# A two-layer decoder trunk on one core: the order and the engines of the block inverses, POOL as a second engine for low parts, halves at the start and in a LayerNorm

## The chip, the cores and the metric

The kernel runs on one core of a Trainium2 chip. The metric is the device time of one execution in microseconds (us). The engines are PE (TensorE, matmuls), DVE (VectorE), ACT (ScalarE), POOL (GpSimd) and SP (SyncE, which here only issues DMAs).

## The reference, cut to what matters

x is 256 tokens of 1024 channels, float32. Layer A is a gated DeltaNet mixer, layer B a MoBA attention; with 256 tokens and blocks of 256 the latter is plain causal attention. Each ends in a LayerNorm over `ALPHA * x + y`.

```python
proj = h @ w_in                                  # q, k, v, z, b, a
qkv = silu(causal_depthwise_conv(qkv, conv_w))   # 4 taps
g = -exp(a_log) * softplus(a + dt_bias);  beta = sigmoid(b)
lower = where(strict, (k_beta @ k.T) * decay, 0.0)
w, u = triangular_solve(eye + lower, ...)        # the inverse that the kernel forms
...                                              # recurrence over chunks of 64
o = o * rsqrt(mean(o**2) + eps) * norm_w * silu(z)
x = layer_norm(ALPHA * x + o @ w_out, g, b)
kb, vb = split(x @ w_kv);  q, z = split(x @ w_in_b)
y = (causal_attention(q, kb, vb) * silu(z)) @ w_out_b
x = layer_norm(ALPHA * x + y, g_b, b_b)
```

## The kernel before, in words

**Weights.** Every weight matrix comes in units of 128 x 1024 numbers (512 KB), 78 of them beside the z columns that the kernel starts with. `load_raw` loads a unit on SP's queue into one of 5 buffers. `high` casts it on ACT to the short format of PE's fast mode (hi); `low` subtracts on DVE (lo = raw - hi), frees the raw buffer and issues the next load. A projection makes three matmuls for each chunk of 128 input channels: hi with hi, hi with the low part of the other operand, lo with hi. `splits` decides when a unit's hi and lo are made, by how far ahead of use they are (RANKS); 9 units of hi and lo are kept. A unit of q, k or v holds one head of 128 columns, and columns 0 to 511 of the unit are its chunks 0 to 3.

**The order of the work.** A planner writes all instructions out at build time. `Clock` keeps a modelled time per engine, for DMA queues and for each tile; `Pipeline` holds chains, generators that yield the engine of their next step and what it needs, and places a step of a chain between the matmuls of the projections when its operands are there in modelled time. On the chip the order of each engine is then fixed, and semaphores carry the real waits. `SPINE` is the order of the projections: z columns 0 to 255 with the gate columns, q and k of 8 heads, v, the rest of z. POOL's two-operand instructions on most tiles are costed at 800 + 190 ns per column, those on tiles named inv at 155 + 1.75 per column.

**Start.** x and the first z columns are loaded in five pieces on two queues (SP, ACT), then the constants, then five raw units. `z_first` multiplies them in plain float32. `x_part` splits x into hi and lo, a piece at a time. `gates` works out g and beta in some twenty short steps on DVE; the products with g (ps_gc) stand in PE's order behind it. `decay` makes the decay matrices E, `conv` the four taps and silu, `gs_head` the products of keys and queries of a head and their scaling into M; POOL stores M to DRAM (md).

**Inverses.** `inverse(grp)` is started for each group of four heads once its four stores are issued. POOL loads the 16x16 diagonal blocks from md to inv, takes a root of the key norms (nk), clears a tile (TR), sets the identity, forms 64 block inverses by 15 steps of a product and a sum, stores them (td), and SP loads them back in eight transfers into TC. Then PE merges the blocks to 32, 64 and 128 with bursts of small matmuls: ps_x and ps_y of 32x32 (64 and 128 matmuls), later larger ones. Between them six copies on POOL bring the 32-blocks into RR and T64. `solve` and `read_out` use the result; og is scaled by zs, the silu of z.

**End of layer A.** The output projection runs by group of heads (`out_half`, k = 0 and 1), token tile t and column half c, in that order; `ln` is added after both halves of t with k = 1: a residual add and bn_stats for each half, bn_aggr, a root on POOL, scaling, shift; `x1_done` transposes on PE and splits x1 into hi and lo, which the values of layer B (`bv`) need.

Of the kernel before, what the change touches and what calls it, by code (L numbers as in the profile page):

```python
# [24 lines left out]
P = 128  # L25
# [21 lines left out]
R_KQ, R_V, R_Z, R_INV, R_SOLVE, R_ATT, R_BZ = 5, 5, 2, 2, 2, 5, 1  # L47
INVERSE = [('gpsimd', 'p'), ('gpsimd', 'p')]
START = 650.0
WARM = 9  # L50
# [59 lines left out]
class Clock:  # L110
# [44 lines left out]
    def note(self, ins):  # L155
# [22 lines left out]
        else:  # L178
# [14 lines left out]
            elif eng == mybir.EngineType.DVE:  # L193
                psum = any(a.tensor.name.startswith("ps_") for a in reads)
                single = ins.opcode in ("TensorCopy", "TensorScalarPtr") and len(reads) - bool(scalars) == 1
                cost = 68 + scalars + n * (6 if ins.opcode == "Reciprocal" else 0.52 if single and not psum else 1.042)
            elif ins.opcode == "TensorTensor":
                cost = 155 + 1.75 * n if ins.outs[0].bass_ap.tensor.name.startswith("inv") else 800 + 190 * n
            else:
                cost = 100 + n  # L200
# [106 lines left out]
def body(ctx, tc, x, xt, cst_in, w0, wp, a_ln_g, a_ln_b, b_ln_g, b_ln_b, out):  # L307
# [45 lines left out]


    specs, idx = [], {}
    for key, _, _, nk, _, n in granules():
# [8 lines left out]
    raws, hls, lows_due = {}, {}, []  # L365
    n_raw, n_split, n_used = [2], [2], [0]

    def load_raw():
        u = n_raw[0]
        raws[u] = rot(wraw, [P, 1024], F32, "raw", f"raw{u}", NR)  # L370
        n_raw[0] += 1
        nc.sync.dma_start(raws[u], wp[u - 2])

# [11 lines left out]
    def low():  # L385

        u, hi, lo = lows_due.pop(0)
        nc.vector.tensor_sub(lo, raws.pop(u), f32(hi))
        if n_raw[0] < len(units):
            load_raw()  # L390

    def rank(u):
# [3 lines left out]
    def splits():  # L396

        r = []
        if lows_due:
            u, hi, _ = lows_due[0]  # L400
            r.append((rank(u), pipe.idle("v") and pipe.there(hi, "v"), low))
        u = n_split[0]
# [62 lines left out]
    alog = cst_sb[:, 105:113].unsqueeze(1)  # L465
    pieces = [slice(0, 1), slice(1, 2), slice(2, 4), slice(4, 6), slice(6, 8)]
    for k in pieces:
        nc.sync.dma_start(x_sb[:, k], xt[:, k])
        nc.scalar.dma_start(zraw[:, k], w0[:, k])
    nc.sync.dma_start(cst_sb, cst_in)  # L470
    for _ in range(NR):
        load_raw()
# [53 lines left out]
    def x_part(hi, lo, raw):  # L526
        yield "a", [raw]
        nc.scalar.copy(hi, raw)
        yield "v", [hi]
        nc.vector.tensor_sub(lo, raw, f32(hi))  # L530

    for k in pieces:
        pipe.add(x_part(xh[:, k], xl[:, k], x_sb[:, k]), 0)
    pipe.others = splits

# [159 lines left out]

    n_md = [0, 0]
    n_gs = [0]
# [6 lines left out]
    def inverse(grp):  # L704
        inv = act.tile([64, 4, 16, 16], F32, tag="ag" if grp == 0 else "ab", name=f"inv{grp}")
        mb, tr, prod = inv[:, 0], inv[:, 1:3], inv[:, 3]
        blk = md[grp, 0, 0:16, 0:16]
        nc.gpsimd.dma_start(mb, bass.AP(tensor=blk.tensor, offset=blk.offset,
                                        ap=[[16 * (P + 1), 64]] + list(blk.ap)))
        nc.gpsimd.tensor_tensor(fl(nk)[:, 8 * grp:8 * grp + 8], fl(ssk)[:, 8 * grp:8 * grp + 8],  # L710
# [9 lines left out]
        nc.gpsimd.memset(t16, 0.0)  # L720
        nc.gpsimd.memset(t16.rearrange("p a b -> p (a b)")[:, 0::17], 1.0)
        eng, e = INVERSE[grp]
        eng = getattr(nc, eng)
        yield e, [inv]
        for j in range(15):
# [5 lines left out]
            if j in (4, 9):  # L731
                yield e, [t16]
        eng.tensor_copy(tr[:, 1], t16.rearrange("p a b -> p b a"))
        yield "p", [inv]
        nc.gpsimd.dma_start(td[grp].rearrange("w q b r c -> (q b) w (r c)"),
                            tr.rearrange("p w r c -> p w (r c)"))
        yield "p", [td[grp]]
        for b in range(8):
            nc.sync.dma_start(TC.rearrange("p w q c -> p (w q) c")[16 * b:16 * b + 16, :, 16 * (b % 2):16 * (b % 2) + 16],
                              td[grp].rearrange("w q b r c -> b r (w q) c")[b])  # L740
# [26 lines left out]
        for b in blocks:  # L767
            nc.gpsimd.tensor_copy(RR[b, :, b], TC[b, 1])
            if b.start < 64:
                nc.gpsimd.tensor_copy(T64[b, :, b], TC[b, 0])  # L770

# [73 lines left out]
    def z_rest(ps, c, t):  # L845
        yield "a", [ps[:, 0:256], lambda: n_E[0] == H]
        nc.scalar.activation(zs[:, t, c * 256:(c + 1) * 256], ps[:, 0:256], AF.Silu)
        end(ps)


# [3 lines left out]
    o_hl = {}  # L854
    n_ro = [0]
    n_s3 = [0, 0]
    n_og = [[0, 0], [0, 0]]
# [36 lines left out]
    def read_out(grp, t, hs, Wg, Z, nw):  # L894
# [20 lines left out]
        nc.gpsimd.tensor_tensor(a, a, nhalf[:, 0:4], op=ALU.pow)  # L915
        yield "v", [a, free("og")]
        og = rot(tmp, [P, 4, P], F32, "og", "og", 2)
# [30 lines left out]
    def z_keep(ps, t):  # L948
        z = zs[:, t, 0:256]
        yield "a", [ps[:, 0:256]]  # L950
        nc.scalar.copy(z, ps[:, 0:256])
        yield "a", [lambda: n_ba[0] == NT]
        end(ps)
        yield "a", [z, lambda: n_E[0] == H]
        nc.scalar.activation(z, z, AF.Silu)

    pipe.add(taps(), 3)
# [104 lines left out]

    oh.g = ol.g = 1
    for t in range(NT):
        pipe.wait(lambda: n_og[1][t])
        for c in range(2):
            pipe.run(out_half("o", 1, ps_y, t, c, oh, ol))
        pipe.add(ln([(ps_y[t, c], halfs[c]) for c in range(2)], halfs, "res", t, "x1", x1_done(t)), 2 + t)

# [166 lines left out]
```

## Time and profile before

| | us |
|---|---|
| median of 3 runs | 306.08 (306.07 to 307.4) |
| profiled execution, its own time | 307.82 |
| its span | 306.1 |
| PE, DVE, ACT, POOL busy | 292.2, 201.8, 162.6, 67.4 |
| granted clock, mean | 0.987 |

The span runs from the first to the last instruction of the profiled execution. Busy time counts neither waits nor the issue of DMAs by SP and ACT. A granted clock of 1.0 is 2.4 GHz, 0.5 is 1.2 GHz. Nearly all instructions are recorded by one helper, line 219, so groups go by the names of tiles.

### The profile page before, as it was taken

What the parts mean: (1) busy time and instruction counts of PE and PEld (TensorE: products, weight loads), DVE (VectorE), ACT (ScalarE), POOL (GpSimd) and SP (SyncE); (2) the same over time, 40 slices, a digit from 0 to 9 for tenths busy, and PEclk for the clock granted to TensorE, in tenths of its full rate; (3) what the DMA queues carried; (4) which work ended last, traced back from release to release, by engine and by line L of the source; (5) the groups of instructions that cost most, each with busy time, mean ns of one, the idle gap of its engine ahead of it and who ended that gap; (6) DMA issues with size and microseconds to landing.
All of it is one profiled execution on the core that took longest, in us unless ns stands there. A gap on an engine that the chain in (4) does not pass through costs nothing. (4 is left out here: it accounts for less than half of the span.)

```text
span 306.1 us, 6559 instructions
## 1 busy us (share of the span) xinstructions
PE 292.2 (95%) x2598; PEld 268.2 (88%) x2598; DVE 201.8 (66%) x432; ACT 162.6 (53%) x327; POOL 67.4 (22%) x137
## 2 busy tenths in 40 slices
PE   7899999999996999999999999999999999999990
PEld 6798988999996999997888678899999999998890
DVE  0589479999995285554455994765655656762645
ACT  2588987556572567455362524875555558561000
POOL 7002410188822988014011110000000000000101
PEclk9999999999999799999999999999999999999996
DMA  6985516565859353433528261796444546400011
GB/s 212 382 306 171 185 34 206 173 204 176 264 139 332 113 158 121 103 114 110 166 98 326 88 206 47 256 317 204 140 132 145 152 160 240 139 0 2 0 69 69
DMA packets 19309, 49.42 MB, mean 161 GB/s; under 512 B 6256, under 2 KB 7152, under 8 KB 19280
## 3 DMA queue, kind: packets, MB, share of 16 engines
q1 hardware_dynamic: 18016, 46.46, 45.8%
q0 software_dynamic: 544, 1.44, 1.8%
q10 hardware_dynamic: 720, 1.11, 1.0%
q8 instruction: 20, 0.33, 0.4%
q14 instruction: 9, 0.07, 0.1%
HBM read 46.65 MB, written 2.36 MB: 160 GB/s over the span
## 5 line engine op out<-in xcount | busy, mean ns | idle before, releaser
L219 DVE TENSOR_TENSOR lo<-raw,hi 128x1024 fp32r<-128x1024 f32 x78 | 95.4, 1230 | 20.9 <-ACT hi L219 20.6
L219 ACT CAST hi<-raw 128x1024 fp32r<-128x1024 f32 x78 | 80.6, 1049 | 15.1 <-DMA raw<-in_wp_dram 7.7
L219 PE MATMUL ps_y<-hi,o 128*128 128x512 f32 (+1 forms) x144 | 43.7, 376 | 0.0
L219 PE MATMUL ps_bkq<-x1h,hi 128*128 128x256 f32 x128 | 38.0, 297 | 0.0
L219 PE MATMUL ps_kq<-xh,hi 128*128 128x256 f32 x128 | 36.7, 287 | 0.0
L219 PE MATMUL ps_kq<-xh,lo 128*128 128x256 f32 x128 | 35.8, 279 | 0.8 <-DVE lo L219 0.8
L219 PE MATMUL ps_kq<-xl,hi 128*128 128x256 f32 x128 | 35.7, 279 | 0.0
L219 PE MATMUL ps_bkq<-x1l,hi 128*128 128x256 f32 x128 | 35.6, 278 | 0.0
L219 PE MATMUL ps_bkq<-x1h,lo 128*128 128x256 f32 x128 | 35.5, 278 | 0.0
L219 POOL TENSOR_TENSOR mv<-mv,nhalf 128x1 f32<-128x1 f32 x4 | 3.8, 952 | 135.3 <-DVE mv L219 135.3
L219 PEld LDWEIGHTS ps_y<-hi,o 128*128 128x128 f32 x144 | 25.9, 188 | 4.8 <-DVE o L219 0.3
L219 PE MATMUL ps_y<-lo,o 128*128 128x512 f32 (+1 forms) x72 | 26.5, 369 | 0.0
L219 POOL TENSOR_TENSOR inv<-inv 64x15 f32<-64x15 f32 (+7 forms) x60 | 24.6, 410 | 4.6
L219 PEld LDWEIGHTS ps_kq<-xh,lo 128*128 128x128 f32 x128 | 24.1, 188 | 1.0 <-DVE lo L219 1.0
L219 PEld LDWEIGHTS ps_kq<-xh,hi 128*128 128x128 f32 x128 | 24.2, 189 | 0.5 <-ACT hi L219 0.3
L219 PEld LDWEIGHTS ps_bkq<-x1h,hi 128*128 128x128 f32 x128 | 24.1, 188 | 0.2
L219 PEld LDWEIGHTS ps_bkq<-x1l,hi 128*128 128x128 f32 x128 | 24.1, 188 | 0.2
L219 PEld LDWEIGHTS ps_bkq<-x1h,lo 128*128 128x128 f32 x128 | 24.1, 188 | 0.0
L219 PEld LDWEIGHTS ps_kq<-xl,hi 128*128 128x128 f32 x128 | 24.1, 188 | 0.0
L219 DVE SCALAR_TENSOR_TENSOR cv<-ps_kq,cst_sb,cv 128x255 f32<-128x255 f32 (+2 forms) x48 | 21.3, 471 | 4.1 <-ACT cv L219 4.0
L219 PE MATMUL ps_v<-xh,hi 128*128 128x256 f32 x64 | 19.0, 297 | 0.0
L219 PE MATMUL ps_bz<-x1h,hi 128*128 128x256 f32 x64 | 18.3, 285 | 0.0
(176 smaller groups left out, 678.7 us busy)
## 6 DMA issues: line engine op xcount, KB each, us to landing
raw<-in_wp_dram SPq DMA_DIRECT2D x78, 512.0 KB, 4.0
md<-ME POOLq DMA_DIRECT2D x8, 128.0 KB, 2.5
late<-in_x_dram SPq DMA_DIRECT2D x1, 1024.0 KB, 6.1
zraw<-in_w_dram ACTq DMA_DIRECT2D x3, 272.0 KB, 5.9
x_sb<-in_xt_dram SPq DMA_DIRECT2D x3, 256.0 KB, 5.2
ag<-in_a_ln_g_dram SPq DMA_DIRECT2D x1, 512.0 KB, 7.0
ab<-in_a_ln_b_dram SPq DMA_DIRECT2D x1, 512.0 KB, 8.3
bg<-in_b_ln_g_dram SPq DMA_DIRECT2D x1, 512.0 KB, 5.5
```

The costliest lines, as they stand in the source:

```text
L219: r = f(*args, **kw)
```

## The change

- **First unit in halves.** Unit 2 (key head 0) is loaded in two halves, ahead of the constants, and split in two halves by a chain of its own (`first_split`, rank 0.5). x and z come in six pieces: chunks 0, 1, 2, 3-4, 5-6, 7.
- **Low parts on POOL.** `low` takes POOL when `spare()` holds: the highs of units 3 and 4 have been made, fewer than three heads' M have been stored, and POOL's modelled time is more than 800 ns behind DVE's. A step on POOL doesn't wait for DVE to be idle. Two-operand instructions of more than 16 columns on POOL are costed like those on inv.
- **Inverses.** The load of the blocks stands behind the root and the clearing on POOL; the store of the result goes from POOL's to SP's queue; of the eight loads back, numbers 2 and 5 go to POOL's queue; the six copies into RR and T64 go to DVE.
- **LN of layer A by halves.** `ln` is added before the output projection of its token tile with a counter, so that the add and statistics of half 0 may stand between the matmuls of half 1.
- **Waits in the planner.** Copying z waits until x is split; scaling og waits for the two z tiles that it reads.

```diff
+LOW_P, LOW_V = 2000, 1200
@@ Clock.note
-                cost = 155 + 1.75 * n if ins.outs[0].bass_ap.tensor.name.startswith("inv") else 800 + 190 * n
+                cost = 155 + 1.75 * n if n > 16 or ins.outs[0].bass_ap.tensor.name.startswith("inv") else 800 + 190 * n
@@ body
-    n_raw, n_split, n_used = [2], [2], [0]
+    n_raw, n_split, n_used = [2], [3], [0]
     def load_raw():
...
-        nc.sync.dma_start(raws[u], wp[u - 2])
+        for c in [slice(0, 512), slice(512, 1024)] if u == 2 else [slice(0, 1024)]:
+            nc.sync.dma_start(raws[u][:, c], wp[u - 2][:, c])
     def low():
         u, hi, lo = lows_due.pop(0)
-        nc.vector.tensor_sub(lo, raws.pop(u), f32(hi))
+        eng = nc.gpsimd if spare() else nc.vector
+        eng.tensor_sub(lo, raws.pop(u), f32(hi))
...
+    def spare():
+        return n_split[0] > 4 and sum(n_md) < 3 and pipe.at("p") + LOW_P < pipe.at("v") + LOW_V
...
-            r.append((rank(u), pipe.idle("v") and pipe.there(hi, "v"), low))
+            r.append((rank(u), (spare() or pipe.idle("v")) and pipe.there(hi, "v"), low))
...
-    pieces = [slice(0, 1), slice(1, 2), slice(2, 4), slice(4, 6), slice(6, 8)]
+    pieces = [slice(0, 1), slice(1, 2), slice(2, 3), slice(3, 5), slice(5, 7), slice(7, 8)]
     for k in pieces:
         nc.sync.dma_start(x_sb[:, k], xt[:, k])
         nc.scalar.dma_start(zraw[:, k], w0[:, k])
+    load_raw()
     nc.sync.dma_start(cst_sb, cst_in)
-    for _ in range(NR):
+    for _ in range(NR - 1):
         load_raw()
...
+    def first_split():
+        for c in (slice(0, 512), slice(512, 1024)):
+            yield from x_part(first_hl[0][:, c], first_hl[1][:, c], raws[2][:, c])
+        raws.pop(2)
+        load_raw()
+    first_hl = [rot(whl, [P, 1024], F32R, w, f"{w}2", NU) for w in ("hi", "lo")]
+    hls[2] = [w.rearrange("p (k n) -> p k n", n=P) for w in first_hl]
+    pipe.add(first_split(), 0.5)
@@ inverse
-        blk = md[grp, 0, 0:16, 0:16]
-        nc.gpsimd.dma_start(mb, bass.AP(tensor=blk.tensor, offset=blk.offset,
-                                        ap=[[16 * (P + 1), 64]] + list(blk.ap)))
         nc.gpsimd.tensor_tensor(fl(nk)[:, 8 * grp:8 * grp + 8], ..., op=ALU.pow)
...
         nc.gpsimd.memset(t16.rearrange("p a b -> p (a b)")[:, 0::17], 1.0)
+        blk = md[grp, 0, 0:16, 0:16]
+        nc.gpsimd.dma_start(mb, bass.AP(tensor=blk.tensor, offset=blk.offset,
+                                        ap=[[16 * (P + 1), 64]] + list(blk.ap)))
...
-        yield "p", [inv]
-        nc.gpsimd.dma_start(td[grp].rearrange("w q b r c -> (q b) w (r c)"),
-                            tr.rearrange("p w r c -> p w (r c)"))
+        yield "t", [inv]
+        nc.sync.dma_start(td[grp].rearrange("w q b r c -> (q b) w (r c)"),
+                          tr.rearrange("p w r c -> p w (r c)"))
         yield "p", [td[grp]]
         for b in range(8):
-            nc.sync.dma_start(TC..., td[grp]...[b])
+            eng = nc.gpsimd if b % 3 == 2 else nc.sync
+            eng.dma_start(TC..., td[grp]...[b])
...
         for b in blocks:
-            nc.gpsimd.tensor_copy(RR[b, :, b], TC[b, 1])
+            nc.vector.tensor_copy(RR[b, :, b], TC[b, 1])
             if b.start < 64:
-                nc.gpsimd.tensor_copy(T64[b, :, b], TC[b, 0])
+                nc.vector.tensor_copy(T64[b, :, b], TC[b, 0])
@@ read_out, z_keep
-        yield "v", [a, free("og")]
+        yield "v", [a, free("og"), lambda: {(2 * grp, t), (2 * grp + 1, t)} <= n_z]
...
-        yield "a", [ps[:, 0:256]]
+        yield "a", [ps[:, 0:256], lambda: n_x[0] == len(pieces)]
@@ the output projection of layer A
+    n_yo = [[0], [0]]
     for t in range(NT):
         pipe.wait(lambda: n_og[1][t])
+        pipe.add(ln([(ps_y[t, c], halfs[c]) for c in range(2)], halfs, "res", t, "x1", x1_done(t), n_yo[t]), 2 + t)
         for c in range(2):
             pipe.run(out_half("o", 1, ps_y, t, c, oh, ol))
-        pipe.add(ln([(ps_y[t, c], halfs[c]) for c in range(2)], halfs, "res", t, "x1", x1_done(t)), 2 + t)
+            n_yo[t][0] += 1
```

## Rows read from the trace of the kernel before

**Rows 1.** The page: busy us of each engine, share of the span, instructions.
```profile
PE 292.2 (95%) x2598; PEld 268.2 (88%) x2598; DVE 201.8 (66%) x432; ACT 162.6 (53%) x327; POOL 67.4 (22%) x137
```
**Rows 2.** Waits of PE: who waited for whom, us in total, times, longest.
```profile
PE ps_y L219 <- issue: 2.5, 1, 2.5
...
PE ps_kq L219 <- DVE lo L219: 0.8, 1, 0.8
PE ps_t L219 <- DVE x L219: 0.6, 1, 0.6
PE ps_gc L219 <- DVE g L219: 0.6, 1, 0.6
```
**Rows 3.** Windows: length, busy us of PE, PEld, DVE, ACT, POOL, clock, DMA share, GB/s.
```profile
24.00:60.00 36.00, 35.55 (x275) 33.12 (x276) 30.03 (x83) 28.65 (x69) 7.92 (x12) 1.00 0.47 149
...
150.00:180.00 30.00, 29.28 (x155) 24.09 (x155) 21.59 (x39) 12.17 (x29) 3.12 (x4) 1.00 0.53 187
```
**Rows 4.** Timeline of the start (start, us, engine, instruction, [idle before]), and its window.
```profile
7.67 5.77 PE L219 MATMUL ps_z<-zraw,x_sb 128*128 128x272 f32 x24 [0.29 <-DMA zraw<-in_w_dram]
...
10.90 0.69 DVE L219 TENSOR_TENSOR xl<-x_sb,xh 128x512 fp32r<-128x512 f32 x1 [0.96 <-ACT xh L219]
...
12.24 1.04 ACT L219 CAST hi<-raw 128x1024 fp32r<-128x1024 f32 x1 [1.38 <-DMA raw<-in_wp_dram]
...
13.34 0.38 PE L219 MATMUL ps_kq<-xh,hi 128*128 128x256 f32 x1
...
14.60 0.38 PE L219 MATMUL ps_kq<-xh,lo 128*128 128x256 f32 x1 [0.76 <-DVE lo L219]
...
7.65:15.30 7.65, 6.87 (x32) 5.48 (x33) 4.43 (x12) 3.87 (x7) 0.00 (x0) 1.00 1.02 382
```
**Rows 5.** Timeline: the second unit's low part and the matmul that first uses it.
```profile
15.05 1.22 DVE L219 TENSOR_TENSOR lo<-raw,hi 128x1024 fp32r<-128x1024 f32 x1
...
17.45 0.28 PE L219 MATMUL ps_kq<-xh,lo 128*128 128x256 f32 x1
```
**Rows 6.** Timeline: residual add and statistics of one half, LayerNorm of layer A.
```profile
165.56 0.69 DVE L219 SCALAR_TENSOR_TENSOR late<-late,ps_y 128x512 f32<-128x512 f32 x1
166.29 0.69 DVE L219 BATCH_NORM_STATS2 st<-late 128x6 f32<-128x512 f32 x1
```
**Rows 7.** Timeline of POOL in the second inverse; waits of POOL and of SP.
```profile
98.48 0.84 POOL L219 DMA_DIRECT2D inv<-md  x1 [5.78 <-DMA md<-ME]
...
103.21 3.14 POOL L219 COPY TR<-TR 32x256 f32<-32x256 f32 x6
...
POOL inv L219 <- DMA md<-ME: 7.8, 2, 5.8
...
SPq L219 <- DVE lo L219: 155.2, 54, 11.0
```
**Rows 8.** Windows around PE's longest wait; loads issued before it; PE's instruction queue.
```profile
97.00:99.50 2.50, 0.02 (x3) 0.00 (x0) 0.00 (x0) 0.00 (x0) 1.01 (x2) 1.00 1.03 398
100.00:103.50 3.50, 3.50 (x45) 3.21 (x44) 0.66 (x1) 2.72 (x6) 3.44 (x5) 0.51 0.21 43
133.00:138.00 5.00, 4.99 (x217) 4.57 (x216) 3.59 (x8) 1.68 (x4) 0.01 (x1) 1.00 0.56 193
...
91.28 3.48 SPq L219 DMA_DIRECT2D raw<-in_wp_dram  x4
...
q8 instruction: 20, 0.33, 0.4%
```
**Rows 9.** Instructions by tile (ns min/median/max, first and last start), and one in the timeline.
```profile
L219 POOL TENSOR_TENSOR inv<-inv x60: 207/282/1306, 68.0 to 120.2; 64x15 f32<-64x15 f32 x8, 64x28 f32<-64x28 f32 x8, 64x39 f32<-64x39 f32 x8, 64x48 f32<-64x48 f32 x8
L219 POOL COPY TR<-TR x12: 389/392/1282, 103.2 to 140.0; 32x256 f32<-32x256 f32 x12
...
L219 DVE TENSOR_TENSOR lo<-raw,hi x78: 1202/1220/1443, 13.3 to 275.4; 128x1024 fp32r<-128x1024 f32 x78
...
117.75 1.18 POOL L219 TENSOR_TENSOR inv<-inv 64x39 f32<-64x39 f32 x1
```

More of the change, by code (lines that the diff above doesn't have):

```diff
@@ L352, in small @@
         return cst.tile(list(shape), F32, name=name)
+    n_md = [0, 0]
     specs, idx = [], {}
@@ L530, in x_part @@
         nc.vector.tensor_sub(lo, raw, f32(hi))
+        n_x[0] += raw.tensor.name == x_sb.tensor.name
+    n_x = [0]
     for k in pieces:
         pipe.add(x_part(xh[:, k], xl[:, k], x_sb[:, k]), 0)
+    def first_split():
[6 more added lines that the diff above has]
+    pipe.add(first_split(), 0.5)
     pipe.others = splits
@@ L694, in gs_head @@
             pipe.add(inverse(h // 4), R_INV)
-    n_md = [0, 0]
     n_gs = [0]
@@ L733, in inverse @@
         eng.tensor_copy(tr[:, 1], t16.rearrange("p a b -> p b a"))
-        yield "p", [inv]
-        nc.gpsimd.dma_start(td[grp].rearrange("w q b r c -> (q b) w (r c)"),
-                            tr.rearrange("p w r c -> p w (r c)"))
+        yield "t", [inv]
+        nc.sync.dma_start(td[grp].rearrange("w q b r c -> (q b) w (r c)"),
+                          tr.rearrange("p w r c -> p w (r c)"))
         yield "p", [td[grp]]
         for b in range(8):
-            nc.sync.dma_start(TC.rearrange("p w q c -> p (w q) c")[16 * b:16 * b + 16, :, 16 * (b % 2):16 * (b % 2) + 16],
+            eng = nc.gpsimd if b % 3 == 2 else nc.sync
+            eng.dma_start(TC.rearrange("p w q c -> p (w q) c")[16 * b:16 * b + 16, :, 16 * (b % 2):16 * (b % 2) + 16],
                               td[grp].rearrange("w q b r c -> b r (w q) c")[b])
@@ L848, in z_rest @@
         end(ps)
+        n_z.add((c, t))
     sso = small("sso", (P, H, NT))
@@ L855, in body @@
     n_ro = [0]
+    n_z = set()
     n_s3 = [0, 0]
@@ L955, in z_keep @@
         nc.scalar.activation(z, z, AF.Silu)
+        n_z.add((0, t))
     pipe.add(taps(), 3)
```

## The prediction

> **What bounds the kernel now.** First view: the page's busy shares [rows 1]. PE is busy 95% of the span, DVE 66%, POOL 22%: the span is TensorE's own work and the holes in it, and a faster other engine is worth only the hole that it closes. So the second view is what PE waited for [rows 2]. Four of its waits lie where the diff reaches: 2.5 us ended by nothing that the profile shows ("issue"), 0.8 for the low part of a weight, 0.6 for an LN result, 0.6 for the gates' g; none names an inverse. The third view is the timeline around each, the fourth the windows, for clock and DMA. In 24 to 60 us PE has 35.55 of 36 us while DVE has 30.03 [rows 3]: DVE is fairly full there, but PE hardly feels it.
>
> **Start-up, part by part.** The z projection starts when its first pieces land; after 8 records PE waits 0.29 us for the piece of two chunks, and from 7.67 it runs without a pause, 24 records up to the first kq matmul at 13.34 [rows 4]. That matmul needs only the high part; its third companion needs the low part and starts at 14.60. That is 1.26 for two spacings that normally take 0.11 to 0.22 each, so 0.9 is lost (0.76 of it shows as idle). The reason is in the same rows: the cast of the whole first unit starts at 12.24, the moment that its load lands, and takes 1.04; DVE's subtraction of such a unit then takes 1.22 [rows 9].
> The change lets chunk 2 come alone: the 0.29 goes if it lands before the eighth record ends (half the bytes of the piece awaited: likely), less what chunk 3, now in the next piece, takes back. I take 0.2 (bounds 0 and 0.3). The first unit's load stands ahead of the constants (56.5 KB) and lands in halves of 256 KB. At the 382 GB/s of that stretch [rows 4] a half is 0.69 us and the constants 0.15, so the first half lands near 12.24 - 0.69 - 0.15 = 11.4. Half a cast is some 0.6 and a subtraction of 512 columns took 0.69 [rows 4]: low part near 12.8, the second half's near 13.4. PE, at about 13.1, wants them at 13.4 and 14.7. So the 0.9 goes. Start-up: -1.1.
> What is late next: the second unit's low part ends at 16.27 and is used at 17.45 [rows 5]. With PE 1.1 earlier its slack is 0.1. It started at 15.05 because the first unit held DVE until just before 14.60, which it no longer does, so I let the gain stand; at worst 0.6 is handed back there and at the third unit. More load issues (two on SP, one on ACT, whose last must wait until an earlier piece has landed) delay ACT's first casts, under cover of the z phase. The copies of z that now wait for all pieces stand behind it too.
>
> **LN statistics by halves.** Before, both halves' residual adds and statistics stand behind the second half's matmuls. With the first half's pair (0.69 + 0.69 [rows 6]) done while the second is multiplied, the chain to the transposes is 1.4 us shorter, more than the 0.6 that PE waits for it [rows 2]. All PE idle time between 150 and 180 us is 0.72 [rows 3], which is the bound; I take -0.7. If splits of the output weights get in between on DVE (1.22 each), it is 0, at worst +0.3.
>
> **Inverses.** In the second one POOL waits 5.78 for the stores, issues the load at 98.48, works until 103.21 on the root and the memsets, and then copies 3.14 for the first group before it multiplies [rows 7]. With the load behind root and memsets these lie inside the wait, and the copies are gone from POOL: 3 us or more earlier. In the first inverse the wait was only 7.8 - 5.8 = 2.0 [rows 7], shorter than the 4 us of work moved ahead of it, so that load is later by up to 2, and the multiplications start about as before. The return loads (six on SP, two on POOL) are a little shorter. PE has no hole that waits for an inverse: 0, and the gain serves as cover for a PE that comes 1.8 earlier. The result's store moves to SP, where weight loads queue behind it until POOL is done; SP already waits up to 11.0 us for a low part [rows 7] without a trace of it at PE, which hides this. Six copies per inverse go to DVE. On POOL they are 0.39 each; if DVE takes as long, 2.4 us in each inverse, on an engine busy 66%: 0.
>
> **Low parts on POOL.** No row shows this shape. POOL's products and sums of 64x15 to 64x64 took 0.207 at least and 0.282 in the median [rows 9]; over some 33 elements that is 2.3 ns each, 2.5 us for 1024. By its copy of 256 elements (0.39) it is 1.6. I take 2.3, nearer to the same operation. The planner counts POOL as taken by its set-up until about 17 us (three adds of 16 columns at 3.84 in its own costs), so POOL comes in from unit 5 or 6 on, until the third head is stored: of some 13 to 16 units I guess nine. DVE is relieved of 9 x 1.22 = 11 us; PE gets 0, since it doesn't wait there. The price: POOL and DVE don't do such work at once. A POOL product that began at 117.75, beside a low part on DVE, lasted 1.18 instead of 0.28, and low parts themselves went from 1.220 up to 1.443 [rows 9].
> The Trainium skill (SBUF — State Buffer, Who interferes with whom) says that a VectorE instruction with two SBUF inputs and a GpSimd instruction that reads SBUF exclude each other for a whole instruction, whichever comes first. The trace agrees, with the 1.18. By it each low part on POOL can hold DVE for its full length instead of 0.2.
> Where this would show is the gates: their steps on DVE are short but have two inputs in SBUF, and PE waits 0.6 for g [rows 2]. Bounds -0.6 and +2.4 (one low part of POOL ahead of the last steps); I take 0, the wait as it is.
>
> **The hole of 2.5 us.** From 97.0 PE, amid the first inverse's bursts of 32x32 matmuls, stands still without any semaphore for 2.48 us; the other engines run dry, and the DMA engines are at 1.03 of their time [rows 8]. The clock then falls to half (0.51 in 100 to 103.5), which costs (1 - 0.51) x 3.5 = 1.7. Together 4.2. The second inverse's bursts (217 matmuls in 133 to 138) pass without it, at a DMA share of 0.56. PE's 5196 instructions came in 20 packets of together 0.33 MB [rows 8], 260 each, and the bursts ps_x and ps_y (192 matmuls, each with its weight load) use up 384 in 4 us. I read it as PE waiting for its next instructions behind the weight loads that SP issues right after the return loads (four in 3.5 us from 91.28). The change touches neither the bursts nor that pile; it moves them by 1 to 3 us. I take 0, bounds -4.2 (gone) and +4.2 (the second inverse's bursts stop too).
> The Trainium skill (Runtime: NRT & Kernel Launch, Instruction fetch mechanics) has instructions refilled in blocks of 16 KiB while the one before runs, and calls this hidden by the rate of issue. The packets agree with the block; that it is hidden disagrees, if my reading holds. By the page the hole would have another cause, which no row names, and the term would be 0 all the same.
>
> **Sum.** -1.1 - 0.7 = -1.8. The profiled execution took 307.82, 1.7 more than its span of 306.1; with the sum it comes to 306.0. The median of the runs shown is 306.08, 1.7 below the profiled execution, so for a timed run: 304.3.
>
> **Rivals.** (a) The hole closes: 304.3 - 4.2 = 300.1. For it: its place hangs on where the bursts fall in the stream of instructions and on DMA engines at 1.03, and both move. Against: the pile of loads follows the return loads as before. (b) A second hole: 304.3 + 4.2 = 308.5, slower than before. Its place is ps_y of the second inverse; it decides once loads at a share near 1 meet that burst, and a store in SP's way can pile them up. Against: 0.56 there now. (c) POOL's low parts block more than they relieve: the gates' +2.4, so 306.7, about as before. For it: the 1.18 beside a low part. Against: the planner starts them late. (d) The change does little of what it says: the start-up hands back its 0.6 and LN gives nothing, 305.6.
>
> **How the numbers follow.** Main case 0.46, its own range 303.0 to 305.4; (a) 0.24; (b) 0.11; (c) 0.11; (d) 0.08. A measurement of this kernel can tell 0.5% (1.5 us) from no change, so the limits are 304.55 and 307.6. Faster: (a) and two thirds of the main case, 0.55. Slower: (b) and the tail of (c), 0.13. Same: 0.32. Range 299.8 to 307.2: it takes in (c), (d) and most of (a), and leaves out (b).
>
> **What would show it.** The first kq matmul near 13.1, and no PE wait for lo behind it; no PE wait for x before the transposes near 169; the root and memsets ahead of the inverse's load on POOL, and in the second inverse the multiplications 3 us or more earlier; low parts on POOL of 2 to 2.5 us between 18 and 55 us; a wait of 2 to 2.5 us put down to "issue" at the first ps_y, with half clock behind it. The last decides most: gone, and I am 4 us too high; twice, and I am 4 too low. Wrong in kind would be PE waits for DVE between 24 and 60 us, where there are almost none.

## The result, and the profile after

The changed kernel took 322.46 us (median of 4 runs) beside 306.74 for the kernel before on the same chip: ratio 1.0515, 95% interval 1.0457 to 1.0573. I had said 304.3 with a range to 307.2. The profiled execution spans 319.3 us against 306.1, 13.2 more.

First the page's busy shares after, the line that answers to [rows 1].

```profile
PE 296.1 (93%) x2598; PEld 273.4 (86%) x2598; DVE 212.4 (67%) x438; ACT 161.8 (51%) x329; POOL 79.5 (25%) x135
```

POOL has 12 us more and DVE 10.6 more, although POOL took eight low parts off DVE. An engine that is busier after it was relieved is being held. The waits of PE after, beside [rows 2]:

```profile
PE ps_g L220 <- ACT kq L220: 6.1, 2, 5.7
PE ps_gc L220 <- DVE g L220: 4.8, 1, 4.8
PE ps_x L220 <- DMA TR<-td: 1.9, 3, 0.9
```

Gone are the 2.5 for "issue" at ps_y, the 0.8 for lo and the 0.6 for x. New are 4.8 for the gates' g, 5.7 for kq, the keys and queries of a later head after convolution and silu, and waits for TR, the first inverse's return loads. Windows over the two large ones and behind them, then the stretches of [rows 3] again (same columns):

```profile
23.40:28.30 4.90, 0.18 (x2) 0.00 (x0) 4.80 (x7) 1.10 (x2) 4.15 (x2) 0.94 0.85 308
27.80:34.50 6.70, 6.14 (x29) 6.17 (x30) 4.13 (x12) 4.06 (x16) 0.77 (x2) 0.50 0.55 174
54.00:59.90 5.90, 0.20 (x2) 0.00 (x0) 5.90 (x11) 0.46 (x2) 2.46 (x2) 0.88 0.60 199
58.50:65.30 6.80, 5.39 (x13) 3.66 (x14) 6.73 (x15) 5.52 (x10) 5.15 (x3) 0.50 0.54 201
...
24.00:60.00 36.00, 25.93 (x182) 24.70 (x182) 24.12 (x49) 20.91 (x55) 15.32 (x15) 0.88 0.37 125
150.00:180.00 30.00, 30.00 (x200) 26.92 (x199) 16.04 (x25) 13.92 (x33) 2.01 (x2) 1.00 0.48 168
```

PE stands still for 4.8 us and again for 5.7; each time its clock is at half afterwards, 0.50 over 6.7 and 6.8 us. PE is busy for 6.14 and 5.39 us of these (the second stretch begins while it still stands), so half clock costs another 3.1 and 2.7. PE's 35.55 of 36 us between 24 and 60 became 25.93.

What DVE and POOL did in the first hole, from their timelines:

```profile
20.97 2.00 DVE L220 SCALAR_TENSOR_TENSOR gpl<-gpl,gs 128x16 f32<-128x16 f32 x1
22.89 0.47 DVE L220 SCALAR_TENSOR_TENSOR cv<-ps_kq,cst_sb,cv 128x255 f32<-128x255 f32 x1
23.29 2.00 DVE L220 SCALAR_TENSOR_TENSOR gpl<-gpl,gs 128x16 f32<-128x16 f32 x1
...
25.60 2.20 DVE L220 SCALAR_TENSOR_TENSOR gpl<-gpl,gs 128x16 f32<-128x16 f32 x2
27.83 0.17 DVE L220 SCALAR_TENSOR_TENSOR gpl<-gy,gpl 128x16 f32<-128x16 f32 x1
...
19.67 7.88 POOL L220 TENSOR_TENSOR lo<-raw,hi 128x1024 fp32r<-128x1024 f32 x3 [12.31 <-ACT hi L220]
```

A step of the gates (16 columns, both inputs in SBUF) takes 0.17 us when POOL is idle, as at 27.83, and 2.0 while POOL subtracts a low part. Three low parts stand back to back from 19.67 to 27.55, and each holds one step (the first of them, itself beside a low part on DVE until 20.57, takes 3.27). The convolution's steps between them (cv), whose first input is in PSUM, keep their 0.47. The second hole:

```profile
50.69 5.18 DVE L220 TENSOR_SCALAR ssk<-ssk 128x2 f32<-128x2 f32 x1
51.13 4.70 POOL L220 TENSOR_TENSOR lo<-raw,hi 128x1024 fp32r<-128x1024 f32 x2
59.44 0.42 ACT L220 ACTIVATE kq<-cv 128x256 f32<-128x256 f32 x1 [7.20 <-DVE cv L220]
```

An addition on two columns takes 5.18 us in place of some 0.15 and ends with the second of POOL's two low parts. It began 0.44 us before the first, while POOL issued a DMA (50.20 to 51.10), so not all of the 5.18 lies beside the low parts. The convolution of the head that PE needs next stands behind it in DVE's order: ACT waits 7.20 us for it, and PE 5.7 for ACT's kq.

The rest, in the order of the prediction. The first low part is used at 13.76 (14.60 in [rows 4]), while the first kq matmul starts at 13.32 and so no earlier than before (13.34); the residual adds and statistics that answer to [rows 6] are

```profile
178.91 0.69 DVE L220 SCALAR_TENSOR_TENSOR late<-late,ps_y 128x512 f32<-128x512 f32 x1 [1.14 <-DMA late<-in_x_dram]
...
180.95 0.69 DVE L220 SCALAR_TENSOR_TENSOR late<-late,ps_y 128x512 f32<-128x512 f32 x1 [0.62 <-PE ps_y L220]
```

POOL in the second inverse, beside [rows 7]:

```profile
104.64 2.14 POOL L220 TENSOR_TENSOR nk<-ssk,half 128x8 f32<-128x8 f32 x1
106.76 1.79 POOL L220 MEMSET TR<- 128x2048 f32 x1
...
109.45 0.86 POOL L220 DMA_DIRECT2D inv<-md  x1 [0.47 <-issue]
112.65 2.51 POOL L220 TENSOR_TENSOR inv<-inv 64x15 f32<-64x15 f32 x8 [2.34 <-DMA inv<-md]
```

Counted from the landing of the group's last store of M (97.95 before, 106.46 here), the multiplications start 8.5 us behind it before and 6.2 here: 2.3 earlier, where I had said 3 or more. POOL's low parts on the page, which [rows 9] could not show, are

```profile
L220 POOL TENSOR_TENSOR lo<-raw,hi 128x1024 fp32r<-128x1024 f32 x8 | 20.6, 2599 | 19.3 <-ACT hi L220 19.2
```

The bookkeeping goes by the same matmuls in both traces: the one with the first low part comes 0.85 us earlier, the one with the third head's first low part 6.50 later (30.07 before), the one with the sixth head's second 14.7 later (57.43 before). So the gates' hole with its slow clock is 7.35 (4.8 + 3.1, less the 0.6 that PE waited for g before) and the second one with its own 8.2 (5.7 + 2.7 would be 8.4); from there to the end 1.5 come back: -4.2 for the hole at ps_y (gone there), +2.9 for the waits at ps_x (1.9 for TR, 1.0 put down to issue), and a small rest. -0.85 + 7.35 + 8.2 - 1.5 = 13.2, the difference of the spans.

### The profile page after: what moved, and what is told of

It is laid out like the page before. It is cut to its first block, busy times and chain, and to the rows that moved or that the text cites. A ratio compares the mean times of both kernels' runs of the same rounds, so it can differ in the third digit from the quotient of the medians.

```text
span 319.3 us, 6596 instructions
## 1 busy us (share of the span) xinstructions
PE 296.1 (93%) x2598; PEld 273.4 (86%) x2598; DVE 212.4 (67%) x438; ACT 161.8 (51%) x329; POOL 79.5 (25%) x135
## 4 chain that ended last, share of the span: by engine, by line
PE 65%; DVE 13%; POOL 6%; DMA 6%; issue 6%; ACT 1%; SPq 1%; ACTq 0%; POOLq 0%; DVEq 0%
PE ps_bkq L220 14%; PE ps_y L220 12%; PE ps_bv L220 7%; PE ps_bz L220 7%; PE ps_z L220 6%; POOL inv L220 4%; PE ps_v L220 3%; PE ps_kq L220 3%; DVE lo L220 3%; DVE ssk L220 3%; DVE gpl L220 2%; PE ps_gb L220 2%; DMA zraw<-in_w_dram 2%; PE ps_o L220 2%; PE ps_s L220 2%
## 5 line engine op out<-in xcount | busy, mean ns | idle before, releaser
L220 DVE TENSOR_TENSOR lo<-raw,hi 128x1024 fp32r<-128x1024 f32 (+1 forms) x71 | 86.9, 1232 | 15.3 <-ACT hi L220 14.9
L220 ACT CAST hi<-raw 128x1024 fp32r<-128x1024 f32 (+1 forms) x79 | 80.5, 1035 | 16.8 <-PE ps_y L220 11.5
L220 PE MATMUL ps_y<-hi,o 128*128 128x512 f32 (+1 forms) x144 | 41.3, 368 | 0.0
L220 POOL TENSOR_TENSOR lo<-raw,hi 128x1024 fp32r<-128x1024 f32 x8 | 20.6, 2599 | 19.3 <-ACT hi L220 19.2
L220 POOL TENSOR_TENSOR inv<-inv 64x15 f32<-64x15 f32 (+7 forms) x60 | 22.6, 376 | 10.1 <-DMA inv<-md 5.7
L220 PE MATMUL ps_g<-kq 128*128 128x512 f32 (+1 forms) x32 | 13.9, 561 | 6.1 <-ACT kq L220 6.1
```

Source lines behind the costliest of these rows:

```text
L220: r = f(*args, **kw)
```

## The experiments

In the experiments' expectations L is the theory that POOL's low parts hold VectorE, O that the order of the inverses costs the time, P that POOL slows VectorE whatever the operands. The kernel before itself lay between 303 and 313 us in these runs, so the time of a single run weighs little and its trace more; e2, e3, e7, e8, e11 and e12 are single runs and not in the table.

| run | us, median | ratio to before, 95% interval |
|---|---|---|
| e1 changed, low parts on VectorE | 317.31 | 1.0288 (1.0201 to 1.0375) |
| e4 start and LN only | 313.33 | 1.0224 (1.0124 to 1.0324) |
| e5 e4 + all bursts spread | 315.72 | 1.0313 (1.0251 to 1.0376) |
| e6 before + all bursts spread | 318.62 | 1.0428 (1.0363 to 1.0494) |
| e9 e4 + first inverse's ps_x later and spread | 310.02 | 1.0082 (1.0045 to 1.0119) |
| e10 e4 + ps_x later alone | 311.29 | 1.0124 (1.0064 to 1.0184) |
| e13 LN alone | 307.55 | 1.0029 (0.9979 to 1.0079) |
| e14 start alone | 308.0 | 1.0042 (1.0003 to 1.0081) |
| e15 LN + first inverse spread | 306.21 | 0.9976 (0.9942 to 1.001) |
| e16 changed, both costly parts undone | 305.26 | 0.9962 (0.9928 to 0.9995) |
| e17 LN + residual's load in two | 305.36 | 0.9971 (0.9931 to 1.001) |
| e18 e16 + residual's load in two, ps_x later, ps_y cut once | 304.37 | 0.9879 (0.983 to 0.9927) |

**Low parts on POOL.** e1 takes them away, e2 adds them alone to the kernel before, e3 puts one operand of the gates' sums in PSUM, e12 cuts each into four.

```
e1   def spare(): return False            # all low parts on VectorE
e2   before + eng = nc.gpsimd if spare() else nc.vector, and what spare() needs
e3   gs2 -> s2 = bank([512], "ps_s2g")[:, 0:16]
e12  for c in four pieces of 256 columns: eng.tensor_sub(lo[:, c], raw[:, c], f32(hi)[:, c])
```

> The changed kernel with every low part on DVE again, all else of the change kept. Theory L (lock): POOL's low parts (2.6 us each) hold DVE's short steps out, gpl 2.0 us instead of 0.17 and ssk 5.18 instead of 0.15; PE waits 4.8 and 5.7 us for them and each wait is followed by 6.8 us of half clock (3.4 us of work). Then both waits go, no half clock before 300 us but where the instruction hole comes back: 300 to 306 us. Rival O (order): the new order, above all the inverses and their transfers on two queues, costs the time, and low parts on POOL cost nothing since PE never waits for lo: stays above 315.

> The kernel before with one part of the change alone, low parts on POOL by the same rule and costs. Theory L: the two long waits of PE (ps_gc for g, ps_g for ssk) appear, each with half clock: 306 + 13 to 17 = 319 to 323 us, less 4 if the instruction hole happens to close. Rival O: 306, within 1.5.

> The changed kernel with low parts on POOL kept, but the gates' s2 lies in PSUM, so that each step gpl<-gpl,s2 has one input in SBUF instead of two. Theory L, in the form that two SBUF inputs are what is locked out: these steps take some 0.17 us beside POOL's low parts, the wait for g falls from 4.8 to under 1 us with its half clock, the wait for ssk stays: 322.5 - 7 = 315, 313 to 317. Rival P: POOL at work slows DVE whatever its operands: gpl stays at 2.0 us and the time at 322. Rival O: no change in time either.

> The changed kernel with each low part on POOL as four subtractions of 256 columns in place of one of 1024. If VectorE gets in between two POOL instructions, no short step of VectorE takes over 1 us, the wait of ps_gc for g falls from 4.8 to under 2, that of ps_g for kq from 6.1 to under 2, and the time is 308 to 317. If POOL keeps VectorE out across instructions that follow each other without a pause, the waits stay as they were and the time is 320 or more.

e1's waits of PE:

```profile
PE ps_x L220 <- DMA TR<-td: 6.7, 3, 5.8
PE ps_x L220 <- issue: 2.4, 1, 2.4
```

The holes for g and kq and the half clock behind them are gone, and PE runs mostly 1.6 to 2.0 us ahead of before from 30 to 86 us. But 317.3 is far from the 300 to 306 that L alone expected: a second cost came out from under the first, a wait for TR of 5.8. O was right on that. e2 (329.26 us, one run) says the same from the other side:

```profile
PE ps_gc L220 <- DVE g L220: 7.5, 1, 7.5
PE ps_kq L220 <- DVE cv L220: 5.9, 1, 5.9
```

Low parts on POOL by themselves cost some 20 us in that run, more than the 13 to 17 expected, and the second wait came at another place, at ps_kq and not at ps_g. e3 (323.66, one run) missed its time and settled the mechanism; its steps beside POOL's three low parts:

```profile
20.98 0.16 DVE L220 SCALAR_TENSOR_TENSOR gpl<-gpl,ps_s2g 128x16 f32<-128x16 f32 x1
...
22.59 0.76 DVE L220 SCALAR_TENSOR_TENSOR gpl<-gpl,gs 128x16 f32<-128x16 f32 x1
23.38 2.27 DVE L220 SCALAR_TENSOR_TENSOR gpl<-gy,gpl 128x16 f32<-128x16 f32 x1
25.68 2.26 DVE L220 TENSOR_TENSOR g<-gpl,ea 128x16 f32<-128x16 f32 x1
...
20.02 7.89 POOL L220 TENSOR_TENSOR lo<-raw,hi 128x1024 fp32r<-128x1024 f32 x3 [12.66 <-ACT hi L220]
```

All six steps with an operand in PSUM took 0.16, four of them while POOL's low part was running (20.98 to 22.55); the next three, with both in SBUF, ran into the low parts instead, so g was as late as before (wait 5.2). That refutes P. e12 (317.54, one run):

```profile
PE ps_gc L220 <- DVE g L220: 3.1, 1, 3.1
...
24.44 0.65 DVE L220 SCALAR_TENSOR_TENSOR gpl<-gy,gpl 128x16 f32<-128x16 f32 x1
25.12 0.65 DVE L220 TENSOR_TENSOR g<-gpl,ea 128x16 f32<-128x16 f32 x1
...
19.82 9.34 POOL L220 TENSOR_TENSOR lo<-raw,hi 128x256 fp32r<-128x256 f32 x12 [12.45 <-ACT hi L220]
```

VectorE does get in between POOL's instructions: no step of the gates took over 0.75 us, about one piece of 0.78. The wait for g fell to 3.1, not to under 2, for nearly every step still meets a piece; that for kq fell from 6.1 to 1.8, with 1.5 more for the squares (sq) behind it.

**The order of the inverses.** e7 puts the change's inverse alone into the kernel before; e11 is e7 with the first load back in front; e8 is e1, so without low parts on POOL, with a truer cost of POOL's products in the planner.

```
e11  if grp == 0: the load of the blocks stands ahead of root and memsets, else behind them
e8   cost of a product on POOL: 155 + 1.75 n  ->  420 + 1.75 n
```

> The kernel before with the change's inverse alone: load behind root and memsets, result stored by SP, loaded back by SP and POOL, small copies on VectorE. Theory T (in the run without POOL's low parts this order cost 5.8 us of PE waiting for TR, with half clock behind it): a PE wait for TR of 2 to 6 us in one of the two inverses, span 309 to 314. Rival: the wait came from the start's 2 us of lead, that is PE was only earlier; then no PE wait for TR over 1 us and a span of 303 to 308, by whether the hole comes.

> The change's inverse alone again, with one thing undone: in the first inverse the load of the blocks stands ahead of root and memsets, as before. If that order cost the wait for TR (load to first product took 6 us wherever it stood, so 3.6 us of set-up ahead of it made the first inverse later), the first product starts at 68 instead of 71.5, the return loads are issued near 90 instead of 93.3, and the wait for TR falls from 5.2 to under 2.5. If the store on SP and the two queues cost it, the wait stays over 4.

> The changed kernel without POOL's low parts, and the planner's cost of a product of the inverse raised by 265 ns, to what a product takes on POOL here (0.39 us in the mean), so that ps_x is placed later. Theory T: the 5.8 us wait for TR goes (under 1.5 us in all), and with it the half clock behind it; what is left is the hole put down to issue (0 to 3 us), span 303 to 309. Rival: the return loads themselves are late (two queues, SP's loads of weights between), so that a wait for TR of over 3 us stays wherever ps_x stands, span over 310.

POOL in the first inverse: the kernel before, then e7, then e11.

```profile
61.98 0.84 POOL L219 DMA_DIRECT2D inv<-md  x1 [2.07 <-DMA md<-ME]
...
67.99 5.28 POOL L219 TENSOR_TENSOR inv<-inv 64x15 f32<-64x15 f32 x12
```

```profile
65.56 0.87 POOL L219 DMA_DIRECT2D inv<-md  x1 [0.47 <-issue]
71.49 1.49 POOL L219 TENSOR_TENSOR inv<-inv 64x15 f32<-64x15 f32 x5 [5.06 <-DMA inv<-md]
```

```profile
62.32 0.84 POOL L219 DMA_DIRECT2D inv<-md  x1 [2.19 <-DMA md<-ME]
...
69.04 4.23 POOL L219 TENSOR_TENSOR inv<-inv 64x15 f32<-64x15 f32 x10
```

From the load to the first product it is 6.0 us before and 5.9 in e7, but not for the same reason. Before, the load landed after 3.2 us (65.20, DMA engines at 0.57 of their time), and POOL's set-up and a store of M, up to 67.96, set the start of the products. In e7 it is issued 3.6 later, behind the set-up, and lands after 5.8 (71.34, DMA engines at 0.72 and then 0.92) with nothing left to hide it, so the products start 3.5 later. In e11 it landed after 3.1. The return loads follow (87.4, 93.3 and 89.4 us), and PE's wait for TR goes 0, 5.2, 1.3. In e7 the clock is at half for 17.1 us from 94.8 on, in which PE is busy for 13.07; that costs another 6.5, more than the wait. The single times: 315.80 for e7, 308.83 for e11. e8 (316.26) kept a wait of 4.5 where I had hoped for under 1.5, for a reason of its own: two of the return loads stand on POOL, and there they came behind the second inverse's products (issued at 105.96, the six on SP at 95.58 to 98.94).

**The hole put down to "issue".** In the kernel before, PE stops behind the 1729th of its recorded instructions (its waits counted; it started at 96.83 us), a packet of 16 KB on its instruction queue begins at 97.34 and ends at 98.31, and PE goes on at 99.51. The traces of e1, e4, e10 and e17 stop behind the very same instruction; the packet starts 0.16 to 0.90 us after the stop and PE resumes 1.5 after it has ended. So do those of e2, e7, e11, e13 and e14 (in all but e13 the packet starts up to 1.1 before the stop), and the changed kernel's, for only 0.45 us (until 112.71). In all eleven PE goes on 1.2 to 1.5 after the packet's end. Other stops put down to issue stand at the 1985th (e18) and the 2753rd (e1, e4, e8, e9, e18), 256 and 1024 instructions further on. So PE was short of instructions. That full DMA engines make the packet late is not shown: in e1 it, too, began only at the stop, with them at 0.65 in the 3 us before. Spreading gives the burst out in pieces with other matmuls between:

```
for q in range(8):
    if q in (2, 4, 6):                       # ps_x; ps_y: every q
        due = pipe.now() + GAP
        yield "t", [lambda: pipe.now() >= due]
```

> As e1, and the inverses as before too: what is left of the change is the start in halves and LN statistics by halves. Theory L: 304 to 305.5 (start -0.9, LN -0.7 to -1.1 against before) if the instruction hole stays as in the kernel before, 300 to 301 if it goes. Rival O: near this too, but e1 far above it.

> The kernel before with the new start and the LN halves (no low parts on POOL, inverses as before), and now the two bursts of 32x32 matmuls of each inverse (ps_x, ps_y) given out a quarter or an eighth at a time with other matmuls between. Theory H (the hole put down to issue is PE short of instructions in a burst): no wait put down to issue over 0.5 us, no stretch at half clock behind it, and with the 1.3 to 2.0 us that the start and the LN gave in the run without the spreading, 301 to 304 us. Rival D (PE stands there because the DMA engines are full, whatever it executes): a hole of 2 to 3 us comes again near the same place, with half clock, 308 to 313 us. Rival W (the spread bursts make the inverse late): waits at ps_z, ps_s1 or ps_vt of several us.

> The kernel before with nothing but the spread bursts of ps_x and ps_y. H: the hole of 2.5 us and the 3.4 us at half clock go, 302 to 304 us, about 4 us less than before. D: same as before within 1 us. W: slower by the wait that comes in.

> The kernel before with the new start and the LN halves; in the first inverse alone the bursts ps_x and ps_y are spread, and ps_x is placed 3.5 us later than the planner would. If the losses of the earlier runs were the wait for TR (PE 2 us early against a POOL that is as late as before), the hole of the first inverse's burst and the second inverse made late by spreading, then none of the three is there: no wait for TR over 0.5 us, no hole put down to issue before 110 us, no half clock behind it, and 301.5 to 304.5 us. If the second inverse is late all the same (its chain ends just ahead of the output projection), waits at ps_og or ps_t of over 1 us and 306 to 312.

> The same without the spreading: ps_x of the first inverse 3.5 us later, in one burst. By the theory that PE runs out of instructions in the burst (the packet with the next ones starts only after PE has stopped), no wait for TR, but a hole of 1 to 3 us at ps_x or ps_y between 93 and 105 us with half clock behind it, 306 to 313. If the hole came only from the weight loads that stood right behind the return loads, the later burst meets emptier DMA engines: no hole, and the same time as the spread one within 1 us.

> LN by halves, and in the first inverse alone the two bursts of 32x32 matmuls spread, more tightly than before (300 ns of the planner's time between pieces). If the hole is PE out of instructions in the burst and nothing else is moved, the hole of 2.5 us and the half clock behind it go: 301 to 304. If main work is used up earlier and the second inverse's chain stands bare at its end, as in the two runs with spreading so far, waits of PE between 125 and 165 us of 2 us and more, and 307 to 311.

Windows: e4 in its hole and behind it; e10 likewise; e15, where nothing stops.

```profile
96.80:99.80 3.00, 0.18 (x20) 0.06 (x7) 0.38 (x1) 0.00 (x0) 0.00 (x0) 0.82 0.94 289
98.80:112.20 13.40, 12.39 (x139) 11.52 (x139) 3.33 (x4) 4.55 (x9) 9.57 (x26) 0.50 0.26 85
```

```profile
96.00:100.00 4.00, 0.90 (x97) 0.78 (x86) 2.60 (x2) 1.21 (x2) 1.79 (x4) 1.00 1.00 399
100.80:111.00 10.20, 10.20 (x118) 9.62 (x117) 3.62 (x7) 3.32 (x8) 8.46 (x25) 0.50 0.24 78
```

```profile
93.00:96.00 3.00, 3.00 (x65) 2.49 (x64) 3.00 (x5) 0.69 (x2) 0.11 (x1) 1.00 0.91 271
96.00:100.00 4.00, 4.00 (x70) 3.52 (x71) 0.75 (x2) 2.79 (x8) 1.57 (x2) 1.00 1.01 398
```

The DMA engines are as full in e15 as in e10 (1.01 and 1.00 of their time); what differs is how fast PE uses up its instructions: in e10 stands a burst, in e15 there is other work between its pieces. In e5, e6, e9 and e15 the first inverse's hole is gone, so rival D falls. None of the four reached its expected time, for spreading is no gift. Each piece costs 0.21 us at its first small matmul and 0.12 at the next large one (0.11 and 0.015 are usual): e15 has ten pieces more than before, some 2 us. And spreading the second inverse too makes it late: e6 waits 2.2 for og and 0.8 for TR, and at 154 us 2.0 put down to issue, where no packet of instructions is late; that one stays unexplained. It is at half clock for 6.7 and 3.3 us behind these. e5 waits 2.2 for TR, 1.5 for x and 1.5 for og. e9 (301.5 to 304.5 expected) has no such wait before 129 us, but then 1.1 put down to issue and 1.8 for a root on POOL (rs), with 3.4 at half clock. So e15 gains 0.2%, which its interval does not tell from nothing, where 4.2 us of hole and slow clock were to be had, and e4, where the hole of 2.8 us stands at the same instruction and the slow clock lasts longer (13.4 us at half), loses 2.2% with the start and the LN in it (1.3% by the medians of the lower times in its series, 312.23 and 308.20).

**Start and LN.**

```
e14  before + the new loads, pieces and first_split()          e13  before + n_yo
e17  e13 + for t in range(NT): nc.sync.dma_start(late["res"][:, t], xv[:, t])
```

> The kernel before with the LN statistics by halves and nothing else; nothing ahead of the output projection changes. If the term of my sum was right, the wait of ps_t for x (0.6 us) goes and the time is 0.5 to 1.2 us below before, ratio 0.996 to 0.998. If DVE is held up elsewhere there (splits of the next weights), within 0.3 us of before.

> The kernel before with the new start-up and nothing else. By the sum, 1.1 us less than before. By the runs so far, the lead of 1.3 to 2 us is there until 85 us and is lost at the first inverse, where PE now comes before the return loads (a wait for TR of 1 to 2 us) and the hole in the burst comes as before or longer: ratio 1.00 to 1.02.

> LN by halves alone, and the residual's load of 1 MB issued as two of 512 KB, the first tile's first. If the load set the time of the first residual add, it starts 1.5 us or more earlier (before 166 us where it was at 167.15), the wait of ps_t for x falls from 1.8 to under 0.7, and the ratio to before is 0.995 to 0.999. If the order of the work on VectorE set it, the wait stays over 1.5.

e14 keeps a lead of 1.7 us until 75 us, then waits 1.8 for TR: PE is early at the first inverse, POOL is not. Nothing is left at the end. In e15, which has the LN halves too, and in e13's trace (309.19 us, one of its longer times), the wait of ps_t for x is 1.8, three times that of before, and VectorE shows why: among its waits in e15, and the first residual add in e17,

```profile
DVE late L220 <- DMA late<-in_x_dram: 1.3, 1, 1.3
```

```profile
165.27 0.69 DVE L219 SCALAR_TENSOR_TENSOR late<-late,ps_y 128x512 f32<-128x512 f32 x1 [1.44 <-DMA late<-in_x_dram]
```

The residual is one load of 1 MB. In the kernel before it is issued at 159.31 and lands at 165.44, and the first residual add of [rows 6] starts at 165.56: that load, not the order on VectorE, is what it waited for. In e15 it landed at 166.56, in e13 at 167.03. In two loads the first half lands at 165.14 (e17), though it was issued 0.9 later than in e15, and PE's wait for x is gone from the list.

**Both costly parts undone, and a better version.** e16 is the changed kernel with low parts on VectorE and the first load in front; e18 adds the residual's load in two, ps_x of the first inverse 2.5 us later, and one cut in its ps_y.

> The changed kernel with its low parts on VectorE and the first inverse's load ahead of root and memsets. If those two parts made up the loss, nothing over 0.3 us is left at the gates, the wait for TR is under 3 us (PE comes 1.8 us early), and the ratio to before is 0.995 to 1.015, by how long the hole and the half clock last. If another part costs (store on SP, two queues, copies on VectorE), the wait for TR stays near the 6.7 us of the run with only the low parts undone, and the ratio is 1.02 or more.

> The change with both costly parts undone, the residual's load in two, ps_x of the first inverse placed 2.5 us later and its ps_y given out in two halves. If PE's wait for TR (2.2 us) and the half clock behind it (3.4 us of it) go and the burst, cut once, leaves time for the next instructions, 302 to 304.5 us, ratio 0.983 to 0.993. If ps_x placed later only makes the rest of the inverse late, or the hole in ps_y comes, 305 to 308.

e16's wait for TR is 2.2 us (6.7 in e1), its ratio 0.9962: so the store on SP, the two queues and the copies on VectorE are not what cost the time there. e18, at 0.9879, is the fastest kernel of the study; the ten lower of before's 17 times in its series have a median of 306.22, by which it is 0.994, so its gain is 0.6 to 1.2%. Its waits of PE, and its window over the first inverse:

```profile
PE ps_y L222 <- issue: 1.4, 1, 1.4
...
PE ps_x L222 <- issue: 0.9, 1, 0.9
PE ps_gc L222 <- DVE g L222: 0.4, 1, 0.4
```

```profile
92.00:105.00 13.00, 11.51 (x331) 10.46 (x330) 8.03 (x15) 6.04 (x11) 6.58 (x18) 0.98 0.82 281
```

PE never waits for TR; two smaller stops put down to issue are left. How much each of e18's three edits gives was not taken apart.

## Why the prediction was wrong

**Low parts on POOL: the step that failed most.** The duration was nearly right (2.3 taken, 2.6 measured) and so was the count (nine, eight). I had the mechanism too, and wrote that by it each low part on POOL can hold VectorE for its full length. But I took 0 at the gates and bounded it by "one low part of POOL ahead of the last steps". It was three in a row, against a chain of dependent steps, of which three each waited until a low part ended: 4.8 at g. The planner's start for POOL, which I put at about 17 us, was the very thing that laid them there (19.67), not what kept them away. And I priced one place only; the second, a two-column addition held for 5.18, cost as much. Both bounds also left out the clock: I had charged half clock behind the hole of 2.5 us, but not behind a wait for g. With it the term was +15.5 (7.35 and 8.2), not 0 to 2.4. PE waits for DVE between 24 and 60 us, my own sign of being wrong in kind, are what came. The Trainium skill (SBUF — State Buffer, Who interferes with whom) says that the pair of ports goes to one instruction as a whole; the 0.17 that became 2.0 agrees, and the 0.16 with one operand in PSUM does too. That page lets a VectorE instruction with two SBUF inputs be shut out, or one in a mode that takes both pairs of ports, and counts tensor_scalar, the kind of the held addition, among those that can enter such a mode; whether the addition was in it no run here tells.

**Inverses: 0, "that load is later by up to 2, and the multiplications start about as before".** Wrong: 3.5 later in e7. POOL's wait of 2.0 in [rows 7] is for the stores, ahead of the load; the load's own way from issue to landing stands in no row there, because the set-up behind it hid it, and I put it at nothing. It was 3.2 us before and 5.8 in e7, where nothing hides it. In the changed kernel (4.1) this lay for the most part under the 15 us that PE was late by then; in e7 it stands bare, a wait of 5.2 with half clock behind it. My cover, a PE with no hole that waits for an inverse, was thin: a PE 1.7 earlier already waits 1.8 (e14).

**LN: -0.7.** In the changed kernel PE's wait of 0.6 for x is gone. Wrong when taken alone: 1.0029, with an interval that excludes little but a gain of over 0.2%. The step that failed is "the chain to the transposes is 1.4 us shorter"; the add at 165.56 stood 0.1 behind the landing of its load, of which the prediction has no row.

**Start-up: -1.1.** Near where it is made (-0.85 at the first low part in the changed kernel, -0.95 to -1.85 in the runs with the new start that keep low parts off POOL, while kernels with the old start differ by up to 0.4 there). The 0.9 of the low part came, the 0.2 of chunk 2 did not show in the changed kernel, and the second unit did not give it back. Wrong at the end: alone it measures 1.0042.

**The hole: 0.** It all but closed, as rival (a) had it, for 4.2: PE still stops at the same instruction, for 0.45 us. Why so little was not tested. Of my reading of its cause, instructions late behind full DMA engines, the first half held in every run that stopped there; the second is not shown, and e1 speaks against it. The Trainium skill (Runtime: NRT & Kernel Launch, Instruction fetch mechanics) calls the refill mostly hidden; here it was not, with PE's packet starting 0.5 us after PE had stopped in the kernel before.

**Rivals and range.** Rival (c) had the right mechanism at 306.7, the price of one low part. A range to 307.2 shut out the case that came about, because each place was priced by one instruction and none with the clock behind it.

## What to carry to other kernels

Before work goes to an idle POOL, list every short VectorE instruction with SBUF operands that will stand beside it, and price each at a whole POOL instruction, times the length of the dependent chain; pieces of a quarter the length, or an operand in PSUM, make that price smaller. A wait of PE costs more than its length where the clock drops behind it: 4.8 us cost 7.9 here, and 5.2 in e7 cost 11.7. A load that no wait shows may be hidden by the work behind it, so before moving that work ahead read the load from issue to landing, and allow for busier DMA engines at the later time; and a lead won at the start is kept only if the next thing that PE meets is earlier too.

## What the hardware showed that I had not expected

- A two-column addition with one SBUF operand was held for 5.18 us, to the end of two low parts on POOL (5.17 in e2 and e3), where steps with two SBUF operands got in between every two (2.0 to 2.3). Between e12's pieces it took 0.50, beside POOL's clearing of TR 1.39 to 1.50 (e1, e7, e8) and beside a DMA issue on POOL 0.38 (before, 43.14).
- PE stops behind the same instruction, the 1729th, in eleven of the twenty traces, and goes on 1.2 to 1.5 us after its next 16 KB have arrived.
- Stretches at half clock behind holes of 2 to 6 us lasted from 3.4 us (before) through 6.7 (changed) and 10.2 (e10) to 13.4 (e4) and 17.1 (e7). A longer hole did not go with a longer stretch: e4 stood 2.8, the changed kernel 4.8 and 5.7.
- A piece of 32x32 matmuls between 128x128 ones costs 0.2 us more than it takes within a burst.
